# Gate and up projection of a decoder layer: 18 of 22 column blocks by seven partial products in place of eight

## The chip, the cores and the metric

The kernel runs on one core of one Trainium2 chip. The metric is the device time of one execution in microseconds, and the median of several runs stands for a kernel. The engines are TensorE (PE; its weight loads are listed as PEld), VectorE (DVE), ScalarE (ACT), GpSimd (POOL) and SyncE (SP), whose queue issues the transfers.

## The reference, cut to what matters

One inference step of a one-layer decoder for a prompt of 512 tokens and a sample group of 8 tokens, so 520 columns in all. The layer projects the normalised input, runs a matrix memory and a windowed attention, mixes them, projects the mix and normalises it. The change lies in what follows:

```python
x = layer_norm(ALPHA * x + mixed @ w_out, ln1_g, ln1_b)
g, u = jnp.split(x @ w_gate_up, 2, axis=-1)        # w_gate_up: 1024 x 5632, float32
ffn = (jax.nn.silu(g) * u) @ w_down                # w_down: 2816 x 1024
ple = jax.nn.sigmoid(x @ w_ple_gate) * (p @ w_ple)
x = layer_norm(ALPHA * x + ffn + ple, ln2_g, ln2_b)
```

All data is float32.

## The kernel before

**Layout.** Activations lie transposed: 128 of the 1024 channels on the partitions, 8 row tiles, 520 token columns. The columns are cut into `HALVES`: 264 (the 8 sample tokens and 256 of the prompt) and 256. A weight piece is 1024 x 128; a transfer of 1 MB brings a block of 256 weight columns, two pieces, into the ring `raw` (two buffers).

**Three products for one.** Every float32 operand is split into a high part (rounded to fp32r) and a low part (the rest). `split` makes the high part with an ACT copy (L190) and the low part with a DVE subtraction (L191). A product is the sum of high x high, high x low and low x high. `mm3` (L200) does that for one half of the columns, `mm3ab` (L217) for both in turn, with 3 x 8 x 2 = 48 matmuls for a piece. Split weights lie in the rings `whi` and `wlo` (three buffers each); `get` prepares pieces two ahead, and when a block's last piece is split, `load_next` asks for another block (L157).

**The stages around the change.** The output projection `w_out_half` runs for each half of the columns; on DVE L1253 and L1254 add the residual, and L1258 sums the rows for the mean. `Ln1` normalises a half: the mean matmul (L1271), `center` (L1277, and squares on ACT, L1282), `accum` (L1287), the variance matmuls (L1294), `rstd`, `diag`, `bcast` (L1317), then `final` (L1326 on DVE, the high part L1328 on ACT) and `final_lo`: for the row tiles in `LN1_POOL` ACT adds the bias into `d` (L1337) and POOL subtracts (L1338), for the others one DVE operation does both (L1340). The normalised activations x1 are `x1hi` and `x1lo`. The second half's normalisation is overlapped with `fill`, which starts the first five gate and up pieces on the first half's columns (L1392), and L1432 then does the first four pieces' other half.

**Gate and up.** There are 11 gate blocks and 11 up blocks, taken in turn: for each b the two gate pieces, then the two up pieces. `ev_g` takes a gate piece out of PSUM (tanh on ACT, L1135, and one DVE operation, L1369), `ev_u` an up piece (the product, L1375, then a split into `hhi`/`hlo`, the operands of the down projection). Then come the gate of the per-layer embeddings (`k_pg`, `base` holds their other factor, read back from `plesc` in one transfer of 2080 KB), the down projection, and the last normalisation with the stores.

**What sets the order.** A planner orders the instructions of each engine by its own model of time, except in the sections `tc.manual_schedule`, whose PE, DVE, ACT and POOL instructions keep the order in which they are written. Ahead of the change there are three such sections: the start, the second half of LayerNorm 1 with the fills, and the end.

Of the kernel before, what the change touches and what calls it, by code (L numbers as in the profile page):

```python
# [33 lines left out]
ALPHA = 2.0 ** 0.25  # L34
LN_EPS = 1e-5
RMS_EPS = 1e-6
KSC = float(P) ** -0.5
ASC = float(HD) ** -0.5
NEG = -1.0e30
# [9 lines left out]
def tile_hybrid_step(  # L49
# [98 lines left out]
    def load_next(part=0, parts=None):  # L148
        i = state["load"]
        if i >= len(blocks):  # L150
            return
        src, kc, ncol = blocks[i]
        if part == 0:
            raws[i] = ring("raw", 2048, 2)[:, : kc * ncol].rearrange("p (k n) -> p k n", k=kc)
        step = P if parts else ncol
        cs = slice(part * step, (part + 1) * step)
        nc.sync.dma_start(raws[i][:, :, cs], src[:, cs].rearrange("(k p) n -> p k n", p=P))  # L157
        if cs.stop >= ncol:
            state["load"] += 1

    def prep_next():
        i = state["prep"]
# [22 lines left out]
    def get(k, ahead=2):  # L185
        prep_to(k + ahead)
        return ready.pop(k)
# [75 lines left out]
    for b in range(4):  # L263
        add_block(w_out2[:, 256 * b : 256 * (b + 1)], KD, 256)
    k_gu = len(pieces)
    for b in range(11):
        add_block(w_gu2[:, 256 * b : 256 * (b + 1)], KD, 256)
        add_block(w_gu2[:, DFF + 256 * b : DFF + 256 * (b + 1)], KD, 256)
    k_pg = len(pieces)
    for b in range(4):  # L270
        add_block(w_pg[0][:, 256 * b : 256 * (b + 1)], KD, 256)
# [924 lines left out]
    for c0, kind, b in wl:  # L1196
        for a in range(2):
            f = 2 * b + a
            if t < 2:
                pa, pb = t01[t]  # L1200
            else:
                kp = kin[t]
                if t == 2:
                    after(prep_to, kp + 2, f_=mid)
                hi, lo = get(kp, 2 if kp + 2 < k_wo else k_wo - 1 - kp)
                pa, pb = psm(), psm()
                mm3ab((pa, pb), [(hi, lo, 0, KD, xhi, xlo, 0)])
            if kind == "qk":
                ev_qk(f, (pa, pb))
                if f == 7:  # L1210
                    G.memset(vaug()[:, :, :, DV : DV + 1], 1.0)
            elif kind == "mv":
                ev_mv(f, (pa, pb))
            elif kind == "k":
                (ev_ak if a == 0 else ev_av)((pa, pb))
            elif kind == "aq":
                ev_aq(f, (pa, pb))
            elif kind in ("mo", "gm"):
                ev_mo(f, (pa, pb))
            elif kind == "ga":  # L1220
                ev_ga(f, (pa, pb))
            sd.run(t)
            if t == 5:
                gates_tile()
            t += 1
        if kind == "gm" and b == 3:
            assert not sd.qs
            p1.__exit__(None, None, None)
            late = ctx.enter_context(tc.tile_pool(name="late", bufs=1))
            TL = [late.tile([P, U], F32, tag=f"L{k}", name=f"L{k}") for k in range(4)]  # L1230

            def sub8(t, k):
                return t[:, k * 1024 : (k + 1) * 1024].rearrange("p (k n) -> p k n", k=KD)

            for k in range(8):
                dest[k_wo + k] = (sub8(TL[k // 4], k % 4), sub8(TL[2 + k // 4], k % 4))

    T5, T6, T7, T8 = TL
    wo = [get(k_wo + k, 0) for k in range(8)]
    dest[k_gu + 3] = (sub8(T7, 0), sub8(T7, 1))  # L1240
    dest[k_gu + 4] = (sub8(T7, 2), sub8(T7, 3))

    rT = [qkT()[:, f, :] for f in range(KD)]
    x1hi, x1lo = xhi, xlo
# [18 lines left out]
    class Ln1:  # L1263
# [66 lines left out]
        def final_lo(self, f):  # L1330
            c0, n = self.c0, self.n
            d = rT[f][:, c0 : c0 + n]
            hi = x1hi[f][:, c0 : c0 + n]
            b1 = vecs[:, V_L1B + f : V_L1B + f + 1]
            lo = rr(x1lo[f][:, c0 : c0 + n])
            if f in LN1_POOL[self.hf]:
                S.activation(d, d, AF.Identity, bias=b1)  # L1337
                G.tensor_tensor(lo, d, hi, ALU.subtract)  # L1338
# [18 lines left out]
    for _ in range(5):  # L1357
        prep_next()

    hhi = [mxhi, mxlo, v3(slab(2))]  # L1360
    hlo = [v3(T5), v3(T6), v3(T7)]
    base4 = v34(late.tile([P, U], F32, tag="L3", name="base"))
    base = [base4[:, f, :] for f in range(KD)]
    nc.sync.dma_start(base4, plesc)

    def ev_g(psx, n):
        th = sig_gate(psx, n)
        t = ring("gt", 264, 5)
        V.scalar_tensor_tensor(t[:, :n], th[:, :n], 1.0, psx[:, :n], ALU.add, ALU.mult)  # L1369
        return t  # L1370

    def ev_u(f, hf, t, psx):
        c0, n = HALVES[hf]
        h32 = ring("tmp", 264, 4)
        V.scalar_tensor_tensor(h32[:, :n], t[:, :n], 0.5, psx[:, :n], ALU.mult, ALU.mult)  # L1375
        split(hhi[f // 8][f % 8][:, c0 : c0 + n], hlo[f // 8][f % 8][:, c0 : c0 + n], h32[:, :n])

    def part(w):
# [5 lines left out]
    with tc.manual_schedule(engines={E.PE, E.DVE, E.Pool, E.Activation}):  # L1384
        n0 = HALVES[0][1]
        pg = [psm() for _ in range(4)]

        def fill(q, k0, k1):
            hi, lo = g0[q]
            for k in range(k0, k1):  # L1390
                for i, (w, a) in enumerate(((hi, x1hi), (hi, x1lo), (lo, x1hi))):
                    T.matmul(  # L1392
                        pg[q][:, :n0], rr(w[:, k, :]), rr(a[k][:, :n0]),
                        start=(k == 0 and i == 0), stop=(k == KD - 1 and i == 2),
                    )
# [44 lines left out]
    for b in range(1, 11):  # L1440
        for a in range(4):
            q = 4 * b + a
            if b == 1 and a == 0:
                pp = (None, psm())
                mm3(pp[1], HALVES[1], part(g0[4]))
                ts[0, 0] = ts.pop((4, 0))
            else:
                w = get(k_gu + q)
                pp = (psm(), psm())
                mm3ab(pp, part(w))  # L1450
            for hf in range(2):
                if pp[hf] is None:
                    continue
                if a < 2:
                    ts[a, hf] = ev_g(pp[hf], HALVES[hf][1])
                else:
                    ev_u(2 * b + a - 2, hf, ts[a - 2, hf], pp[hf])

    for f in range(KD):
        w = get(k_pg + f)  # L1460
        p2 = (psm(), psm())
        mm3ab(p2, part(w))
        for psx, (c0, n) in zip(p2, HALVES):
# [232 lines left out]
```

## Time and profile before

| what | value |
|---|---|
| runs | 922.14, 919.64, 918.80 us; median 919.64 |
| profiled execution | 920.83 us, span 918.9 us, mean granted clock 0.989 |
| PE busy | 897.4 us, 98%, 7342 matmuls |
| DVE, ACT, POOL busy | 59%, 43%, 17% |
| transfers | 99.39 MB, mean 108 GB/s |

How to read the profile's lines: `L217` is line 217 of the kernel; `out<-in` names tiles with their buffer numbers left out (`psm` and `pss` are the two PSUM rings of four banks, `T` the large activation buffers, `L` the late ones); then the shape, the count, the busy time in us and the mean of one in ns. In a timeline the columns are the start and the length in us, and the square bracket gives the idle time ahead of an instruction on its engine and what ended it. Neighbouring instructions of one kind are merged.

### The profile page before, as it was taken

How to read it: one execution, taken by the hardware profiler on the slowest of the kernel's cores; microseconds unless marked ns; L12 is line 12 of the kernel's file. 1: busy time of each engine (PE TensorE's matmuls, PEld its weight loads, DVE VectorE, ACT ScalarE, POOL GpSimd, SP SyncE). 2: the span in 40 equal slices, each digit the busy share in tenths (PEclk: the TensorE clock that was granted, in tenths of full speed). 3: DMA queues.
4: the chain of work that ended last, by engine and by line, in shares of the span. 5: the costliest groups of instructions: out<-in, count | busy, mean ns of one | idle time of the engine just before them, and what ended most of it. 6: DMA issues, size and time to landing. Idle time of an engine off the chain costs nothing.

```text
span 918.9 us, 18329 instructions
## 1 busy us (share of the span) xinstructions
PE 897.4 (98%) x7342; PEld 885.6 (96%) x7342; DVE 545.5 (59%) x1367; ACT 397.5 (43%) x926; POOL 159.3 (17%) x320
## 2 busy tenths in 40 slices
PE   8999999999999999999999999999999999999994
PEld 7899999999999999999999999999999999999994
DVE  6788565788887768787875433333333355233327
ACT  5545355668777655565335222222222222122212
POOL 5441321125555211210022000000000000000004
PEclk9999999999999999999999999999999999999997
DMA  7542721544656431124421222222222223322212
GB/s 234 192 163 69 212 72 58 99 96 124 204 164 206 116 92 48 48 91 140 137 93 46 93 93 93 93 92 93 92 93 92 93 92 109 110 89 96 64 41 93
DMA packets 97731, 99.39 MB, mean 108 GB/s; under 512 B 5434, under 2 KB 93202, under 8 KB 97496
## 3 DMA queue, kind: packets, MB, share of 16 engines
q1 hardware_dynamic: 97216, 96.94, 34.0%
q8 instruction: 57, 0.93, 0.4%
q10 hardware_dynamic: 432, 1.31, 0.4%
q14 instruction: 26, 0.21, 0.1%
HBM read 89.01 MB, written 10.34 MB: 108 GB/s over the span
## 4 chain that ended last, share of the span: by engine, by line
PE 90%; DVE 5%; DMA 2%; ACT 1%; issue 1%; SPq 0%; POOL 0%; DVEq 0%; ACTq 0%
PE psm L217 69%; PE psm L200 6%; PE pss L650 2%; PE pss L703 1%; PE psm L1392 1%; PE pss L687 1%; PE psm L434 1%; PE pss L1036 1%; PE pss L1040 1%; DMA big<-vsd 1%; PE pss L1114 1%; PE pss L1432 1%; PE psm L1432 1%; DMA T<-in_w_ple_dram 1%; PE pss L1038 1%
## 5 line engine op out<-in xcount | busy, mean ns | idle before, releaser
L217 PE MATMUL psm<-T,whi 128*128 128x256 f32 (+1 forms) x3236 | 547.2, 284 | 0.0
L217 PEld LDWEIGHTS psm<-T,whi 128*128 128x128 f32 x3236 | 454.0, 188 | 1.9 <-PE pss L1114 0.3
L217 PE MATMUL psm<-T,wlo 128*128 128x264 f32 (+1 forms) x1716 | 362.9, 286 | 0.0
L217 PEld LDWEIGHTS psm<-T,wlo 128*128 128x128 f32 x1716 | 269.0, 188 | 0.6
L190 ACT ACTIVATE whi<-raw 128x1024 fp32r<-128x1024 f32 (+1 forms) x122 | 127.4, 1045 | 317.7 <-PE psm L217 258.6
L191 DVE TENSOR_TENSOR wlo<-raw,whi 128x1024 fp32r<-128x1024 f32 (+1 forms) x122 | 148.5, 1217 | 191.8 <-ACT whi L190 185.9
L1490 POOL COPY T<-tmp 128x8 f32<-128x8 f32 x8 | 1.5, 190 | 401.4 <-DVE tmp L1488 401.4
L217 PE MATMUL psm<-L,whi 128*128 128x264 f32 (+1 forms) x308 | 61.9, 282 | 0.0
L675 POOL TENSOR_SCALAR g<-g,sm 128x256 f32<-128x256 f32 (+1 forms) x64 | 37.2, 594 | 81.3 <-DVE sm L673 24.1
L1375 DVE SCALAR_TENSOR_TENSOR tmp<-gt,psm 128x264 f32<-128x264 f32 (+1 forms) x44 | 16.9, 421 | 57.6 <-PE psm L217 57.6
L200 PE MATMUL psm<-T,L 128*128 128x256 f32 (+1 forms) x280 | 49.5, 283 | 0.0
L217 PEld LDWEIGHTS psm<-L,whi 128*128 128x128 f32 x308 | 47.2, 188 | 0.0
L200 PEld LDWEIGHTS psm<-T,L 128*128 128x128 f32 x280 | 42.5, 188 | 0.0
L668 ACT ACTIVATE g<-g,sm 128x256 f32<-128x256 f32 (+1 forms) x64 | 30.2, 474 | 18.9 <-DVE sm L664 17.8
L1135 ACT ACTIVATE th<-psm 128x264 f32<-128x264 f32 x106 | 35.4, 378 | 5.5 <-DVE T L1142 2.4
L200 PE MATMUL psm<-S,L 128*128 128x264 f32 (+1 forms) x128 | 36.3, 286 | 0.0
L191 POOL TENSOR_TENSOR gt<-big,gt 128x256 fp32r<-128x256 f32 x32 | 27.6, 872 | 48.7 <-ACT gt L190 34.2
L659 DVE CUSTOM_DVE_ANT_0 g<-pss,amaskA,sink 128x256 f32<-128x256 f32 (+1 forms) x64 | 26.2, 446 | 4.6 <-PE pss L650 3.0
L217 PE MATMUL psm<-S,whi 128*128 128x264 f32 (+1 forms) x144 | 28.4, 288 | 0.0
L217 PE MATMUL psm<-S,wlo 128*128 128x264 f32 (+1 forms) x128 | 26.0, 285 | 0.0
L200 PEld LDWEIGHTS psm<-S,L 128*128 128x128 f32 x128 | 24.0, 188 | 0.0
L703 PE MATMUL pss<-big,VS 128*128 128x256 f32 x112 | 23.4, 304 | 0.0
(362 smaller groups left out, 1249.0 us busy)
## 6 DMA issues: line engine op xcount, KB each, us to landing
raw<-in_w_in_dram SPq DMA_DIRECT2D x24, 1024.0 KB
raw<-in_w_gate_up_dram SPq DMA_DIRECT2D x22, 1024.0 KB
raw<-in_w_down_dram SPq DMA_DIRECT2D x6, 1024.0 KB
big<-in_state_mlstm_C_dram SPq DMA_DIRECT2D x8, 512.0 KB
big<-vsd SPq DMA_DIRECT2D x8, 512.0 KB
out_dram<-big SPq DMA_DIRECT2D x8, 512.0 KB
raw<-in_w_out_dram SPq DMA_DIRECT2D x4, 1024.0 KB
raw<-in_w_ple_gate_dram SPq DMA_DIRECT2D x4, 1024.0 KB
```

What stands on the lines that cost most here:

```text
L190: S.activation(rr(hi), src, AF.Copy)
L191: (le or V).tensor_tensor(rr(lo), src, hi, ALU.subtract)
L200: T.matmul(ps[:, :n], rr(w[:, k, wc : wc + P]), rr(a[k0 + k][:, c0 : c0 + n]), start=(i == 0), stop=(i == tot - 1),)
L217: T.matmul(ps[:, :n], rr(w[:, k, wc : wc + P]), rr(a[k0 + k][:, c0 : c0 + n]), start=(i == 0), stop=(i == tot - 1),)
L650: T.matmul(sc[:, a, :w], rr(q[:, a, n * P : (n + 1) * P]), rr(KS[:, kv, hl, (n - 1 + k0) * P : (n + 1) * P]), start=(hl == 0), stop=(hl == 1),
L659: V.tensor_tensor_reduce(out=pr[:, a, :w], in0=sc[:, a, :w], in1=amaskA[:, k0 * P :], scale=1.0, scalar=sink8[:, 2 * j + a : 2 * j + a + 1 ...
L668: S.activation(pr[:, a, :w], pr[:, a, :w], AF.Exp, bias=sm[:, 2 + a : 3 + a], scale=ASC, accum_out=sm[:, 8 + a : 9 + a],)
L675: G.tensor_scalar(pr[:, a, :w], pr[:, a, :w], sm[:, 12 + a : 13 + a], 0.5, ALU.mult, ALU.mult)
L703: T.matmul(po[:, :256], rr(VS[:, n - 1 + k0 + b, kv, :]), rr(pp[:, x, b, :]), start=(i == 0), stop=(i == 2 * kb - 1),)
L1135: S.activation(th[:, :n], psx[:, :n], AF.Tanh, scale=0.5)
L1375: V.scalar_tensor_tensor(h32[:, :n], t[:, :n], 0.5, psx[:, :n], ALU.mult, ALU.mult)
L1432: T.matmul(pb4[q][:, :n1], rr(w[:, k, :]), rr(a[k][:, c1 : c1 + n1]), start=(k == 0 and i == 0), stop=(k == KD - 1 and i == 2),)
```

## The change

The gate and up blocks with b = 2 to 10, 18 blocks of 256 weight columns, are computed by one level of Strassen's algorithm in Winograd's form. The weight block is cut into 2 x 2 parts of 512 x 128, the activations into 2 x 2 parts of 512 channels x 260 columns. Seven products of these parts (12 matmuls of 260 columns each: 4 row tiles, 3 terms) replace eight. For each weight block DVE makes four sums of parts of 512 columns, and seven parts are split into high and low. The sums of x1 are made once, in place, and split (`TSTEPS`), written in block b = 1; for that `final_lo` leaves the whole of x1 in `d` for every row tile, with the bias added by ACT.

Partial results that two outputs share aren't added up on DVE: ACT copies a finished partial sum from one PSUM bank into another (a seed), and the next product accumulates on it. In the first two blocks one priming matmul goes ahead of a seed in each of the two banks concerned.

The loop over the 126 products is a section ordered by hand. In each iteration it writes the low part for four products ahead, the weight sum for six ahead, pending low parts of results, the harvest of the last product, seeds, the high part for five ahead, transfers, pending ACT work, and then the product. The products of one block overlap those of the next: s4 and a22 of a block come among the first of the next one.

Further edits: `ev_g` uses Silu on ACT alone, and `ev_u` a plain product; the weight blocks arrive as four transfers of 256 KB into slots of the two `raw` buffers; the last six tiles of the gated result stay unsplit until the `k_pg` stage; `base` comes back in eight transfers after the loop; two more row tiles of the fills (and the rest of the first piece) stand ahead of the mean matmul.

```diff
+BSW = 2
+TH = NT // 2
...
+    def st_load(g, n):
+        i = {"a11": 2 * g % 3, "a12": (2 * g + 1) % 3, "a21": 3 + g % 2, "a22": 5 + g % 3}[n]
...
+        nc.sync.dma_start(dst, sw[g][0][k0 * P : (k0 + 4) * P, c0 : c0 + P].rearrange("(k p) n -> p k n", p=P))
...
-            if f in LN1_POOL[self.hf]:
-                S.activation(d, d, AF.Identity, bias=b1)
-                G.tensor_tensor(lo, d, hi, ALU.subtract)
-            else:
-                V.scalar_tensor_tensor(lo, d, b1, hi, ALU.add, ALU.subtract)
+            S.activation(d, d, AF.Identity, bias=b1)
+            (G if f in LN1_POOL[self.hf] else V).tensor_tensor(lo, d, hi, ALU.subtract)
...
     def ev_g(psx, n):
-        th = sig_gate(psx, n)
         t = ring("gt", 264, 5)
-        V.scalar_tensor_tensor(t[:, :n], th[:, :n], 1.0, psx[:, :n], ALU.add, ALU.mult)
+        S.activation(t[:, :n], psx[:, :n], AF.Silu)
...
-        fill(0, 0, 5)
+        fill(0, 0, 8)
+        fill(1, 0, 2)
         lb.mean(accB)
-        fill(0, 5, 8)
+        fill(1, 2, 8)
...
-        fill(1, 0, 8)
...
+    TSTEPS = (
+        [(tsum, 0, j) for j in J4] + [(tsplit, 0, j) for j in J4] + [(tsum, 2, j) for j in J4],
+        [(tsum, 1, j) for j in J4] + [(tsplit, 1, j) for j in J4],
+        [(tsplit, 2, j) for j in J4] + [(tsum, 3, j) for j in J4],
+        [(tsplit, 3, j) for j in J4],
+    )
...
+    ORDER = (("a11", 0), ("s4", 1), ("s1", 0), ("s2", 0), ("a22", 1), ("a12", 0), ("s3", 0))
...
+    def w_sum(i):
+        g, form = steps[i]
+        if form in WBLK:
+            r = blk(g, form)
+        elif form == "s1":
+            r, s2f[g] = (ring("stg", NT, 2)[:, :512].rearrange("p (k n) -> p k n", k=4) for _ in range(2))
+            V.tensor_tensor(r, blk(g, "a21"), blk(g, "a22"), ALU.add)
+            V.tensor_tensor(s2f[g], blk(g, "a11"), r, ALU.add)
...
+    def prod(ps, g, form, start=True):
+        hi, lo = wf.pop((g, form))
+        xh, xl = TF[form]
+        for j in range(4):
+            for i, (w, x) in enumerate(((hi, xh), (hi, xl), (lo, xh))):
+                T.matmul(
+                    ps[:, :TH], rr(w[:, j, :]), rr(x[j]), start=(start and j == 0 and i == 0),
+                    stop=(j == 3 and i == 2), skip_group_check=not start,
+                )
...
+        if form == "a11":
+            pb, pa = pss(), pz[g, "a"]
+            pz[g, "b"] = pb
+            if g < 2:
+                prime(pb)
+            seed(lambda: S.activation(pb[:, :TH], pa[:, :TH], AF.Copy))
...
+    AHEAD = 5
+    ns = len(steps)
+    with tc.manual_schedule(engines={E.PE, E.DVE, E.Pool, E.Activation}):
+        for s in range(-AHEAD - 1, ns + 3):
+            if 0 <= s + AHEAD - 1 < ns:
+                w_lo(s + AHEAD - 1)
+            if s + AHEAD + 1 < ns:
+                w_sum(s + AHEAD + 1)
+            do(s, "dve")
+            if 0 < s <= ns:
+                harvest(s)
+            do(s, "seed")
+            if 0 <= s + AHEAD < ns:
+                w_hi(s + AHEAD)
+            elif ns - 3 <= s < ns:
+                prep_next()
+            st_loads(s)
+            do(s, "act")
+            if 0 <= s < ns:
+                product(s)
```

More of the change, by code (lines that the diff above doesn't have):

```diff
@@ L151, in load_next @@
             return
+        if blocks[i] is None:
+            state["load"] += 1
+            st_begin(i - k_sw)
+            return
         src, kc, ncol = blocks[i]
@@ L1358, in tile_hybrid_step @@
         prep_next()
[L1360 to L1364, printed above, removed]
+    hhi = [mxhi, mxlo]
+    hlo = [v3(T5[0]), v3(T6[0])]
     def ev_g(psx, n):
-        th = sig_gate(psx, n)
         t = ring("gt", 264, 5)
-        V.scalar_tensor_tensor(t[:, :n], th[:, :n], 1.0, psx[:, :n], ALU.add, ALU.mult)
+        S.activation(t[:, :n], psx[:, :n], AF.Silu)
         return t
@@ new lines, in tile_hybrid_step, with blk @@
+    ORDER = (("a11", 0), ("s4", 1), ("s1", 0), ("s2", 0), ("a22", 1), ("a12", 0), ("s3", 0))
+    steps = []
+    for g in range(len(sw) + 1):
+        for form, back in ORDER:
+            if 0 <= g - back < len(sw):
+                steps.append((g - back, form))
+    wf, s2f, nslot = {}, {}, [0]
+    wsrcs = {}
+    def blk(g, n):
+        return wblk[g, n]
+    def w_sum(i):
[6 more added lines that the diff above has]
+            V.tensor_tensor(s2f[g], blk(g, "a11"), r, ALU.add)
+        elif form == "s2":
+            r = s2f[g]
+        elif form == "s3":
+            r = blk(g, "a21")
+            V.tensor_tensor(r, blk(g, "a11"), r, ALU.add)
+        else:
+            r = blk(g, "a12")
+            V.tensor_tensor(r, r, s2f.pop(g), ALU.add)
+        wsrcs[i] = r
@@ new lines, in w_hi, with w_lo, st_loads @@
+    def w_hi(i):
+        nslot[0] += 1
+        t = ring(("whi", "wlo")[nslot[0] % 2], 1024, 3).rearrange("p (x k n) -> p x k n", x=2, k=4)
+        wf[steps[i]] = t[:, 0], t[:, 1]
+        S.activation(rr(t[:, 0]), wsrcs[i], AF.Copy)
+    def w_lo(i):
+        g, form = steps[i]
+        hi, lo = wf[g, form]
+        V.tensor_tensor(rr(lo), wsrcs.pop(i), hi, ALU.subtract)
+    def st_loads(s):
+        s += 2
+        for n, o in (("a22", 14), ("a21", 12), ("a11", 10), ("a12", 7)):
+            g = (s + o) // 7
+            if (s + o) % 7 == 0 and g < len(sw) and (g, n) not in wblk:
+                st_load(g, n)
+        if s in (7 * (len(sw) - 1) + 1, 7 * len(sw) + 1):
+            load_next()
@@ new lines, in prod, with prime @@
+    def prod(ps, g, form, start=True):
[7 more added lines that the diff above has]
+                )
+    def prime(ps):
+        T.matmul(ps[:, :TH], rr(x1hi[0][:, :P]), rr(x1hi[0][:, :TH]), start=True, stop=True)
@@ new lines, in tile_hybrid_step, with later, put_g, silu @@
+    todo = {}
+    def later(s, kind, f):
+        todo.setdefault((s, kind), []).append(f)
+    def put_g(s, b, r, hf, src, sc=1.0, own=None):
+        t = own or ring("gt", 264, 5)
+        ts[r, hf] = t
+        def silu():
+            S.activation(t[:, :TH], src, AF.Silu, scale=sc)
+        later(s if own is None else s + 1, "act", silu)
+    def put_h(s, b, r, hf, src, sc=1.0, own=None):
+        t = ts.pop((r, hf))[:, :TH]
+        f, c0 = 2 * b + r, hf * TH
+        if f >= 16:
+            h = h6[f - 16][:, c0 : c0 + TH]
+        else:
+            h = (own or ring("tmp", 264, 4))[:, :TH]
+        V.scalar_tensor_tensor(h, src, sc, t, ALU.mult, ALU.mult)
+        if f < 16:
+            hi, lo = (x[f // 8][f % 8][:, c0 : c0 + TH] for x in (hhi, hlo))
+            later(s + 1, "act", lambda: S.activation(rr(hi), h, AF.Copy))
+            later(s + 2, "dve", lambda: V.tensor_tensor(rr(lo), h, hi, ALU.subtract))
@@ new lines, in tile_hybrid_step, with product @@
+    pz = {}
+    def product(s):
+        g, form = steps[s]
+        if form == "a11":
+            pz[g, "a"] = psm()
+            prod(pz[g, "a"], g, form)
+        elif form == "s1":
+            pz[g, "c"] = pss()
+            prod(pz[g, "c"], g, form)
+        elif form == "s2":
+            prod(pz[g, "b"], g, form, start=False)
+        elif form == "a12":
+            prod(pz[g, "a"], g, form, start=False)
+        elif form == "s3":
+            prod(pz[g, "d"], g, form, start=False)
+        elif form == "s4":
+            prod(pz[g, "c"], g, form, start=False)
+        elif form == "a22":
+            prod(pz[g, "d"], g, form, start=False)
@@ new lines, in do @@
+    def do(s, kind):
+        for f in todo.pop((s, kind), ()):
+            f()
+    AHEAD = 5
[18 more added lines that the diff above has]
+                product(s)
```

125 lines of the change are left out of this document (116 added, 9 removed).

## The prediction, made before the changed kernel was built or run

> **What bounds the kernel now.** First the page: busy shares, and the slices of the span.
>
> ```profile
> span 918.9 us, 18329 instructions
> PE 897.4 (98%) x7342; PEld 885.6 (96%) x7342; DVE 545.5 (59%) x1367; ACT 397.5 (43%) x926; POOL 159.3 (17%) x320
> ...
> DVE  6788565788887768787875433333333355233327
> ACT  5545355668777655565335222222222222122212
> POOL 5441321125555211210022000000000000000004
> PEclk9999999999999999999999999999999999999997
> ```
>
> PE is busy 98% of the span; from the 23rd slice on, where the change lies, DVE stands at 3 tenths and ACT at 2. Busy matmuls alone prove little, since they are pipelined, so next comes the chain that ended last, in order of time, and the busy time in chosen stretches.
>
> ```profile
> 421.74 27.42 PE psm L200 x226
> 449.61 10.08 PE psm L200 x85
> ...
> 499.68 2.84 PE psm L200 x24
> 502.52 301.14 PE psm L217 x2507
> ```
>
> ```profile
> 464.00:475.00 11.00, 9.15 (x75) 8.89 (x74) 9.96 (x22) 5.56 (x14) 4.06 (x5) 1.00 0.36 126
> 485.00:502.00 17.00, 17.00 (x146) 17.00 (x145) 7.47 (x16) 10.94 (x24) 6.04 (x8) 1.00 0.01 1
> 547.00:593.00 46.00, 46.00 (x385) 46.00 (x384) 18.25 (x32) 13.17 (x24) 0.00 (x0) 1.00 0.28 93
> 856.00:887.00 31.00, 31.00 (x261) 31.00 (x260) 10.05 (x18) 7.26 (x11) 0.38 (x2) 1.00 0.26 77
> 887.00:919.00 32.00, 19.46 (x153) 18.21 (x152) 19.38 (x47) 6.58 (x13) 9.87 (x11) 0.80 0.18 67
> ```
>
> (Columns: stretch, its length, busy PE, weight load, DVE, ACT, POOL, granted clock, DMA share, GB/s.) From 502.52 on the chain is one unbroken run of matmuls: 301.14/2507 = 120.1 ns each, at 260 columns on average (264 and 256 in turn). In 547:593 PE never idles and DVE has 28 us of 46 free. So here a removed matmul is worth 120.1 ns, as long as DVE and ACT can feed PE.
>
> **The change, part by part.**
>
> *Matmuls.* A block of 256 weight columns takes 2 pieces x 48 = 96 matmuls of 260 columns on average. Seven products of 4 row tiles x 3 terms make 84 of 260. 18 blocks x 12 fewer = 216, x 120.1 ns = -25.9 us. Four priming matmuls come back: +0.5. That each matmul now has weights of its own costs nothing: L200 in the rows above runs one half at a time, with new weights for each matmul, at 121.3 ns (264 columns) and 118.6 (256), mean 120.0. The Trainium skill (TensorE: Matmul & The Clock Gate, Back-to-back issue gap) gives N/2.4 + 2.5 ns for a warm matmul by itself, an estimate of 110.8 ns at 260 columns; by it the 216 would be worth 23.9 us. The rows measure 9 ns more, and the sum goes by them.
>
> *The loop's DVE and ACT work.* Prices:
>
> ```profile
> L390 DVE TENSOR_TENSOR g<-T,g 128x512 fp32r<-128x512 f32 x2 | 1.3, 696 | 0.0
> L1375 DVE SCALAR_TENSOR_TENSOR tmp<-gt,psm 128x264 f32<-128x264 f32 x22 | 9.4, 427 | 57.6 <-PE psm L217 57.6
> L387 ACT ACTIVATE g<-T 128x512 fp32r<-128x512 f32 x2 | 1.1, 618 | 0.0
> L1135 ACT ACTIVATE th<-psm 128x264 f32<-128x264 f32 x54 | 20.3, 378 | 2.6 <-PE psm L217 2.1
> L190 ACT ACTIVATE T<-tmp 128x264 fp32r<-128x264 f32 x14 | 5.7, 410 | 1.1 <-DVE tmp L1375 1.1
> L131 ACT ACT_TABLE_LOAD x1 | 1.3, 1283 | 0.7 <-PEq L1683 0.7
> ```
>
> ```profile
> 40.28 0.69 DVE L390 TENSOR_TENSOR g<-T,g 128x512 fp32r<-128x512 f32 x1
> ...
> 40.89 0.70 DVE L390 TENSOR_TENSOR g<-T,g 128x512 fp32r<-128x512 f32 x1
> ...
> 561.04 1.23 DVE L191 TENSOR_TENSOR wlo<-raw,whi 128x1024 fp32r<-128x1024 f32 x1 [0.21 <-ACT whi L190]
> 562.19 0.76 DVE L191 TENSOR_TENSOR L<-tmp,T 128x264 fp32r<-128x264 f32 x2
> ```
>
> Durations overlap their neighbours: two 264-wide operations take 0.76 us, so the second adds 0.34, and two 512-wide ones start 0.61 apart. A gate block and its up block together need on DVE: 14 low parts and 8 weight sums of 512, and of 260 columns 2 combinations for the gate, 2 combinations, 4 products and 4 low parts for up: 22 x 0.61 + 12 x 0.34 = 17.5 us (22 x 0.696 + 12 x 0.427 = 20.4 if nothing overlapped). PE needs 168 x 0.1201 = 20.2 us for the pair. ACT: 14 x 0.618 + 12 x 0.378 (8 seeds and saved copies, 4 Silu) + 4 x 0.410 = 14.8. So DVE goes from 4 tenths to about 87%, near the limit but under it, and 4 operations lighter in the last three up blocks, which leave the split for later.
>
> The cover is the order. Low parts are issued four products ahead of their matmuls: 4 x 12 x 0.1201 = 5.8 us. The worst stretch on DVE is the first four products after an up block: 4 low parts, 4 weight sums and about 6 operations of 260 columns: 8 x 0.61 + 6 x 0.34 = 6.9 us against 5.8 us of PE. The lag of 1.1 us fits into the lead, and the next three products (4.3 us) carry only about 2.5 us. Each iteration issues the weight work ahead of the harvest, the operation that waits for PE; behind a waiting harvest stands the next low part, with those four products in hand. A seed is read by the second or third product after it: 2.9 us for a copy that the trace has only from PSUM into SBUF (0.38); PSUM to PSUM I take as that; at 0.618, the dearest copy above, it is still in time, and a cheaper one gains nothing. On ACT, too, the seed waits for PE with the high part for five products ahead behind it. Stalls inside the loop: 0 to 2, I take 0.5.
>
> *Weight loads.* The same bytes arrive as 72 transfers of 256 KB with 512-byte rows in place of 18 of 1 MB with 1024-byte rows, 1 MB per 10.1 us = 104 GB/s. With 1024-byte rows 93 GB/s took a share of 0.28; in 856:887, which fetches the 128-column blocks of w_down in 512-byte rows, 77 GB/s took 0.26. By that 104 GB/s take 0.35. A block is asked for at least five iterations (7.2 us) before its high part is made, and SP has only these transfers to issue. Nothing on the path; a late one would stop ACT's queue first, PE four products later.
>
> *Silu for tanh and one DVE operation.* It frees DVE, which was not the bound: 0. It adds at most one table load, 1.28 us, on ACT about 479, where ACT then waits until 485.33 (next fence): 0, or +1.3 without that cover.
>
> *LayerNorm 1 and the fills.*
>
> ```profile
> 469.83 0.40 PE L1392 MATMUL psm<-T,whi 128*128 128x264 f32 x2
> ...
> 470.32 2.54 POOL L1338 TENSOR_TENSOR T<-T,T 128x264 fp32r<-128x264 f32 x3 [1.27 <-ACT T L1337]
> ...
> 469.74 1.32 ACT L1337 ACTIVATE T<-T,vecs 128x264 f32<-128x264 f32 x3
> ...
> 485.33 1.31 ACT L1328 ACTIVATE T<-T,vecs 128x256 fp32r<-128x256 f32 x3 [5.92 <-DVE T L1326]
> ```
>
> ```profile
> 473.65 0.70 PE L1271 MATMUL pss<-gt,onesD 128*128 128x256 f32 x2 [1.85 <-DVE gt L1258]
> ...
> 478.56 0.83 DVE L1287 TENSOR_TENSOR gt<-gt,tmp 128x256 f32<-128x256 f32 x2 [0.21 <-ACT tmp L1282]
> ...
> 481.10 0.95 PE L1294 MATMUL pss<-onesD,gt 128*128 128x1 f32 x8
> ```
>
> PE stood idle 1.85 us ahead of the mean (the only idle in 464:475). 15 more matmuls (1.82 us) now precede it. Three additions on ACT (0.41 us apart) put the last high and low parts of half 0 back by 1.2 us, to 472.3 on ACT and about 473.1 after POOL, so fill 0, which reaches its last row tile at 469.83 + 21 x 0.121 = 472.4, may wait some 0.6 us there; the mean comes 0.45 us later and PE has 1.82 us more behind it: -1.4 (ends -1.85 and 0). The variance then is reached 1.4 us earlier, at 479.8, about when its squares are summed (479.4 + 0.45): the slack of 1.7 us is used up, and nothing later than this sum becomes late.
>
> *Sums and splits of x1, and the way into the loop.* 16 sums and 16 low parts on DVE, 32 x 0.34 = 10.9 us, and 16 copies on ACT, 6.6 us. They go into the idle 9.5 us of DVE in 485:502 and the 3.5 pieces after it (20.2 us, with some 12 us of work of their own). Whether the planner may slip them between instructions of a section ordered by hand shows at 32 us:
>
> ```profile
> 32.12 0.41 DVE L359 TENSOR_TENSOR T<-tmp,T 128x256 fp32r<-128x256 f32 x1
> ...
> 32.58 1.63 DVE L191 TENSOR_TENSOR wlo<-raw,whi 128x1024 fp32r<-128x1024 f32 x1
> 34.13 0.48 DVE L354 CAST T<-tmp 128x256 fp32r<-128x256 f32 x2
> ```
>
> L359 and L354 belong to such a section, L191 doesn't, so it may; the first splits of the loop can likewise run beside the last pieces. If not, the 20 sums and low parts written ahead of the third piece's split cost 20 x 0.34 - 2.84 (the half piece that PE still has) = 4.0 us. Ends 0 and +4; I take +1, nearer the rows above.
>
> *The way out.* Three preparations in the last three iterations, eight loads of 260 KB in place of one of 2080, six splits of 520 columns (0.7 us on DVE) beside pieces of 5.8 us: hidden; ends 0 and +2, taken +0.5. The tail is the same.
>
> Sum: -25.9 + 0.5 + 0.5 - 1.4 + 1.0 + 0.5 = -24.8. The profiled execution took 920.83 (span 918.9 and 1.93 around it), 1.19 over the median of the three runs; 919.64 - 24.8 = 894.8.
>
> **The rivals.**
>
> *DVE becomes the bound.* If durations don't overlap, a pair takes 20.4 against 20.2: +2 us in nine pairs, 897. If in addition each of the 12 narrow operations waits 0.21 us for its releaser, as at 561.04, a pair takes 22.9: +24 us, and nothing is gained. Against it: that wait ended a copy issued immediately before, while here one iteration lies between. Middle: 906.
>
> *The x1 work blocks the way in.* +4 us, and up to 2 more for the first low parts of the loop: 899.
>
> *Slower: pauses between products bring down the granted clock.* The last row of the stretches has PE busy 19.46 of 32 us and the clock at 0.80. At 0.80 the loop's 1512 matmuls (181.6 us) would take 227: +45, 940. It decides below a clock of 0.88 over the loop. Against it: in 485:502 PE went round four banks in groups of three matmuls with 17.00 us busy of 17.00 and the clock at 1.00. The Trainium skill (TensorE: Matmul & The Clock Gate, A second HAM failure mode: psum-queue depth-cycling) warns of just this, short idles between groups that cycle through the banks. By that row the trace doesn't bear it out, so its chance is small.
>
> *The change doesn't do what it says: a matmul costs more than 120 ns.* Its moving columns now start at multiples of 1040 bytes; all starts so far were multiples of 32 bytes, so no row shows it. 6 ns each cost 9 us (904); at 16 ns the gain is gone.
>
> **How the numbers follow.** Forecast 0.62 (own range 892 to 897); way in 0.15; DVE bound 0.14; dearer matmuls 0.04; clock 0.05. The range: 891, the floor of the sum (919.64 - 25.9 + 0.5 - 1.85 = 892.4) and 1 us of spread between runs, to 906, which takes in the way in and half of the DVE case: about 0.82. A change of 0.5% (4.6 us) is about what can be told from none. Faster 0.90 (the first three but the upper end of DVE, and most of the fourth), same 0.04, slower 0.06 (clock, and the dearest matmuls).
>
> **What would show it.** Right: some 216 fewer matmuls net of the primes, 120 ns each in the loop, PE full and the clock at 1.00 there, DVE 8 to 9 tenths, no idle ahead of the mean matmul. Wrong: PE idle released by a DVE low part inside the loop (DVE the bound), idle about 502 to 520 released by DVE (way in), matmuls over 125 ns, or a clock under 1.00.

## The result, and the profile after

The changed kernel takes 897.88 us (median of 4 runs) against 920.68 before (4 runs, the three of the table and one more); the ratio is 0.9756, with a 95% interval from 0.9725 to 0.9788. The forecast was 894.8, in a range from 891 to 906. The profiled execution took 900.21 us, its span 898.2.

The page of the changed kernel, lines as shown of before:

```profile
span 898.2 us, 18486 instructions
PE 873.0 (97%) x7130; PEld 860.3 (96%) x7130; DVE 637.4 (71%) x1547; ACT 466.6 (52%) x1102; POOL 159.2 (18%) x320
...
DVE  7788555688888777778877978999988654223327
ACT  6545254657777655557326656666665522212212
POOL 5441321115464411311014100000000000000004
PEclk9999999999999999999999999999999999999997
```

DVE now stands at 7 to 9 tenths in the slices of the loop, ACT at 5 to 6; the granted clock reads as before. The chain that ended last, in order of time, from the way into the loop to the way out:

```profile
503.89 1.04 ACT whi L216
505.20 0.95 ACT whi L216
506.87 1.15 DVE wlo L217
508.06 17.28 PE psm L243 x142
525.34 1.43 PE psm L1600 x12
526.89 2.88 PE pss L1600 x24
...
704.23 1.45 PE pss L1600 x12
705.68 1.69 PE psm L243 x14
707.37 1.45 PE psm L1600 x12
708.82 74.58 PE psm L243 x621
```

L1600 is the matmul of the seven products (`prod`). From 525 to 709 the chain is PE alone, as it was before; 14 matmuls of the next stage (1.69 us) have slipped in ahead of the last product. Outside it, one stretch of ACT and DVE stands on the chain at 504 to 508: the way into the loop. A window inside the loop (columns as above):

```profile
530.00:700.00 170.00, 170.00 (x1420) 170.00 (x1419) 150.65 (x276) 110.96 (x246) 0.00 (x0) 1.00 0.37 106
```

PE has no idle, DVE is busy for 89%, ACT for 65%. (The last three pairs of blocks, which leave the split for later, begin in this window. Four full pairs, 565.94 to 646.54, take 80.60 us, with DVE busy for 73.16: 18.3 us of 20.15 for a pair.)

Since the start of the program varies from execution to execution (last section), the comparisons below measure from the first fill matmul (469.83 us before, 474.24 after) to the end of the span: the **stretch**. It took 449.07 us before and 423.96 after: 25.1 us less. Ahead of it this execution lost 4.4 us, and the spans differ by the rest, 20.7. The parts, in us:

| part of the stretch | before | after |
|---|---|---|
| first fill matmul to the second half's matmuls | 18.41 | 17.78 |
| second half's matmuls | 11.28 | 11.28 |
| from there to the first product (before: 24 + 144 matmuls, 2.84 + 17.29) | 20.13 | 21.87 |
| from there to the end | 399.25 | 373.03 |

### The profile page after: what moved, and what is told of

The parts are those of the page before. It is cut to its first block, busy times and chain, and to the rows that moved or that the text cites. A ratio compares the mean times of both kernels' runs of the same rounds, so it can differ in the third digit from the quotient of the medians.

```text
span 898.2 us, 18486 instructions
## 1 busy us (share of the span) xinstructions
PE 873.0 (97%) x7130; PEld 860.3 (96%) x7130; DVE 637.4 (71%) x1547; ACT 466.6 (52%) x1102; POOL 159.2 (18%) x320
## 4 chain that ended last, share of the span: by engine, by line
PE 85%; DVE 6%; DMA 3%; ACT 3%; issue 1%; POOL 1%; SPq 0%; DVEq 0%; ACTq 0%; POOLq 0%
PE psm L243 46%; PE psm L1600 12%; PE pss L1600 9%; PE psm L226 6%; PE pss L683 2%; DMA big<-vsd 1%; PE psm L467 1%; PE pss L736 1%; PE pss L720 1%; PE psm L1428 1%; PE pss L1069 1%; PE pss L1073 1%; ACT T L1371 1%; DMA out_dram<-stg 1%; DMA T<-in_w_ple_dram 1%
## 5 line engine op out<-in xcount | busy, mean ns | idle before, releaser
L243 PE MATMUL psm<-T,whi 128*128 128x264 f32 x2000 | 346.5, 286 | 0.6 <-DVE Qbd L670 0.4
L243 PEld LDWEIGHTS psm<-T,whi 128*128 128x128 f32 x2000 | 284.7, 189 | 2.6 <-PE pss L1147 0.6
L243 PE MATMUL psm<-T,wlo 128*128 128x264 f32 (+1 forms) x1056 | 230.0, 288 | 1.5 <-DVE wlo L217 1.5
L217 DVE TENSOR_TENSOR wlo<-raw,whi 128x1024 fp32r<-128x1024 f32 (+1 forms) x86 | 104.8, 1218 | 107.2 <-ACT whi L216 106.8
L243 PEld LDWEIGHTS psm<-T,wlo 128*128 128x128 f32 x1056 | 168.1, 189 | 2.4 <-DVE wlo L217 1.7
L216 ACT ACTIVATE whi<-raw 128x1024 fp32r<-128x1024 f32 (+1 forms) x86 | 89.1, 1038 | 154.5 <-PE psm L243 139.6
L243 PE MATMUL psm<-L,whi 128*128 128x264 f32 x224 | 45.0, 282 | 0.0
L1584 DVE TENSOR_TENSOR whi<-raw,whi 128x512 fp32r<-128x512 f32 x45 | 30.9, 687 | 8.5 <-ACT whi L1579 7.6
L1584 DVE TENSOR_TENSOR wlo<-raw,wlo 128x512 fp32r<-128x512 f32 x45 | 30.9, 686 | 3.7 <-ACT wlo L1579 3.3
L1600 PE MATMUL psm<-tf,whi 128*128 128x260 f32 x228 | 30.3, 282 | 0.0
L1600 PE MATMUL psm<-T,wlo 128*128 128x260 f32 x216 | 28.9, 283 | 0.0
L1600 PE MATMUL pss<-tf,whi 128*128 128x260 f32 x216 | 28.9, 283 | 0.0
L1600 PE MATMUL pss<-tf,wlo 128*128 128x260 f32 x216 | 28.9, 283 | 0.0
L1600 PE MATMUL psm<-T,whi 128*128 128x260 f32 x216 | 28.9, 283 | 0.0
```

The lines of the kernel that those rows point to most:

```text
L216: S.activation(rr(hi), src, AF.Copy)
L217: (le or V).tensor_tensor(rr(lo), src, hi, ALU.subtract)
L243: T.matmul(ps[:, :n], rr(w[:, k, wc : wc + P]), rr(a[k0 + k][:, c0 : c0 + n]), start=(i == 0), stop=(i == tot - 1),)
L1584: V.tensor_tensor(rr(lo), wsrcs.pop(i), hi, ALU.subtract)
L1600: T.matmul(ps[:, :TH], rr(w[:, j, :]), rr(x[j]), start=(start and j == 0 and i == 0), stop=(j == 3 and i == 2), skip_group_check=not start,)
```

## The experiments

The table gives the four parts for every run, as the timelines of their traces have them; its first column is where the stretch began.

| run | begins | to second half | second half | to first product | from there | stretch |
|---|---|---|---|---|---|---|
| before | 469.83 | 18.41 | 11.28 | - | - | 449.07 |
| changed | 474.24 | 17.78 | 11.28 | 21.87 | 373.03 | 423.96 |
| silu_only | 470.71 | 18.41 | 11.28 | - | - | 448.79 |
| ten_blocks | 473.07 | 17.78 | 11.29 | - | - | 435.83 |
| preps_first | 470.01 | 17.79 | 11.28 | 20.11 | 373.01 | 422.19 |
| fills_old | 470.79 | 17.27 | 11.28 | 21.91 | 372.95 | 423.41 |
| dve2 | 471.02 | 17.75 | 11.28 | 21.89 | 373.36 | 424.28 |
| dve4 | 473.26 | 17.78 | 11.28 | 21.88 | 396.80 | 447.74 |
| ahead3 | 472.77 | 17.77 | 11.28 | 21.90 | 372.88 | 423.83 |
| ahead2 | 471.06 | 17.79 | 11.28 | 21.88 | 373.09 | 424.04 |
| ahead1 | 474.00 | 17.77 | 11.28 | 21.91 | 401.74 | 452.70 |
| ln1_only | 474.91 | 17.29 | 11.28 | - | - | 448.09 |
| both_edits | 473.78 | 17.28 | 11.29 | 20.11 | 373.04 | 421.72 |
| after_again | 473.44 | 17.80 | 11.28 | 21.90 | 372.98 | 423.96 |

Where an edit doesn't touch a part, that part repeats within 0.1 us (from the first product on within 0.25): differences far below the spread of whole runs can be read here. The span is read to 0.1 us, so the last two columns are good to 0.05. The ratios below are each against runs of before made beside them. `fills_old`, `ln1_only`, `dve2`, `dve4` and `ahead1` to `ahead3` are one execution each; of them only the parts are compared.

**Is the gain the removed matmuls?** Two runs: one part of the change alone in the kernel before, and the whole change with fewer blocks.

```diff
     def ev_g(psx, n):
-        th = sig_gate(psx, n)
         t = ring("gt", 264, 5)
-        V.scalar_tensor_tensor(t[:, :n], th[:, :n], 1.0, psx[:, :n], ALU.add, ALU.mult)
+        S.activation(t[:, :n], psx[:, :n], AF.Silu)
...
-        V.scalar_tensor_tensor(h32[:, :n], t[:, :n], 0.5, psx[:, :n], ALU.mult, ALU.mult)
+        V.tensor_tensor(h32[:, :n], t[:, :n], psx[:, :n], ALU.mult)
```

> The kernel before with one part of the change alone: Silu in place of tanh and a DVE operation, in all 22 blocks. Theory (PE is the bound, DVE had room): the time from the first fill matmul to the end of the span stays at 449 us, give or take 0.5, and the ratio to before is 1.000. Rival (part of the gain comes from DVE operations saved): that stretch is 2 us or more shorter.

Measured: ratio 0.9995 (0.9973 to 1.0017), stretch 448.79, 0.3 less than before. That 0.3 lies at the very end: from the tenth-last matmul to the end of the span it is 12.55 us before (12.68 in `ln1_only`), and 12.24 to 12.31 in every run with Silu; the cause is open. Up to there fewer DVE operations are worth nothing: DVE had room.

```diff
-BSW = 2
+BSW = 6
```

> The changed kernel with 10 blocks by seven products in place of 18; the other 8 go by eight products. Theory (the gain is 12 matmuls of 120 ns per block, 1.44 us, on top of costs that don't depend on the number of blocks): the stretch from the first fill matmul to the end is 8 x 1.44 = 11.5 us longer than the 424.0 of the changed kernel, 435.5, and the time is near 909. Rival (the loop pays per block for stalls, or the gain lies elsewhere): the difference is clearly under 11.5 us, and the time stays under 905.

Measured: 911.27 us, 2 more than the 909 expected, ratio 0.9859 (0.9838 to 0.9879); stretch 435.83 against the 435.5 expected, 11.9 longer than with 18 blocks, 1.48 us for each of the eight. The gain goes by blocks, at the price of 12 matmuls each (1.44). The remaining 13.2 us of gain are 10 blocks at that price less the costs that don't grow with their number.

**The way into the loop.** PE's timeline in the changed kernel:

```profile
506.14 0.40 PE L243 MATMUL psm<-T,whi 128*128 128x264 f32 x2
508.06 0.39 PE L243 MATMUL psm<-T,wlo 128*128 128x264 f32 x1 [1.52 <-DVE wlo L217]
```

The piece's first two terms need only the high part; the third waits for the low part. DVE had worked from 488.6 on without a pause, most of it on sums and low parts of x1. The edit queues the later ones behind this piece's split:

```diff
             if b == BSW - 1:
+                if a == 0:
+                    prep_to(k_gu + 5)
+                    first = list(last_split)
                 for f, i, j in TSTEPS[a]:
-                    f(i, j)
+                    if a == 0:
+                        f(i, j)
+                    else:
+                        after(f, i, j, f_=first)
```

(`last_split` holds the two instructions of the last split, and `after` orders what follows behind them.)

> The changed kernel with the split of the sixth gate and up piece written ahead of the sums and splits of x1, and the last 20 of the sums and low parts queued behind it. Theory (PE's idle at 506 us, which ends with that piece's low part, comes from the x1 work ahead of it on DVE and ACT): the idle of 1.5 us goes and the stretch from the first fill matmul to the end is 1.5 to 1.9 us shorter, 422.3. Rival (the piece waits for its buffers or its weights): the idle stays.

Measured: the wait is gone, and the part takes 20.11 us, the time of its 168 matmuls; the stretch is 1.77 us shorter. The time is 895.39 us, ratio 0.9695 (0.9673 to 0.9717). Its DVE timeline has the split first:

```profile
499.24 1.23 DVE L217 TENSOR_TENSOR wlo<-raw,whi 128x1024 fp32r<-128x1024 f32 x1 [2.13 <-PE psm L1470]
500.38 1.44 DVE L1493 SCALAR_TENSOR_TENSOR T<-T 128x260 f32<-128x260 f32 x4
```

The split did wait for a buffer, until matmuls of the second half (L1470) let it go, but its low part then began 2.7 us ahead of the piece's first matmul (501.92). So the buffers and the weights are there in time; the order of the x1 work was the cause.

**LayerNorm 1 and the fills.**

```diff
-        fill(0, 0, 8)
-        fill(1, 0, 2)
+        fill(0, 0, 5)
         lb.mean(accB)
-        fill(1, 2, 8)
+        fill(0, 5, 8)
...
+        fill(1, 0, 8)
```

> The changed kernel with the fills around the mean matmul in their old order (five row tiles ahead of it). Theory (the new order hides the wait for the sum of rows): PE idles ahead of the mean matmul again by 1 to 2 us, and the start of the second half's matmuls comes 0.5 to 1.5 us later after the first fill matmul than the 17.7 us of the changed kernel. Rival (the sum is in time either way): no change.

The expectation failed. The second half's matmuls start 17.27 us after the first fill, 0.5 earlier than in the changed kernel, and PE waits only 0.33 us ahead of the mean, for a low part and not for the sum. The two PE timelines, changed kernel and old order:

```profile
474.24 0.40 PE L1428 MATMUL psm<-T,whi 128*128 128x264 f32 x2
...
476.43 0.40 PE L1428 MATMUL psm<-T,whi 128*128 128x264 f32 x1 [0.31 <-POOL T L1380]
...
477.31 0.39 PE L1428 MATMUL psm<-T,whi 128*128 128x264 f32 x1 [0.25 <-POOL T L1380]
...
479.29 0.59 PE L1314 MATMUL pss<-gt,onesD 128*128 128x256 f32 x2
```

```profile
472.97 0.39 PE L1428 MATMUL psm<-T,whi 128*128 128x264 f32 x1 [0.33 <-POOL T L1380]
473.20 0.29 PE L1428 MATMUL psm<-T,wlo 128*128 128x264 f32 x1
473.32 0.63 PE L1314 MATMUL pss<-gt,onesD 128*128 128x256 f32 x2
```

With the new order PE meets two late low parts (0.56 us of idle) ahead of the mean, and the mean comes 5.05 us after the first fill in place of 2.53: 30 matmuls precede it, which alone take 30 x 0.121 = 3.6 us, in place of 15. So something else had taken away the old wait of 1.85 us. The kernel before with the LayerNorm edit alone tells what:

```diff
-            if f in LN1_POOL[self.hf]:
-                S.activation(d, d, AF.Identity, bias=b1)
-                G.tensor_tensor(lo, d, hi, ALU.subtract)
-            else:
-                V.scalar_tensor_tensor(lo, d, b1, hi, ALU.add, ALU.subtract)
+            S.activation(d, d, AF.Identity, bias=b1)
+            (G if f in LN1_POOL[self.hf] else V).tensor_tensor(lo, d, hi, ALU.subtract)
```

> The kernel before with one part of the change alone: in LayerNorm 1 ACT adds the bias for every row tile and the low part is a plain subtraction. Theory (the plain subtraction and the planner's new order on DVE, not the order of the fills, bring the sum of rows earlier): the sum is ready about 2.4 us after the first fill matmul in place of 3.8, and the second half's matmuls start 17.3 us after it in place of 18.4. Rival (the order of the fills was needed): 18.4 or more.

Measured: 17.29 and, from its DVE timeline, a sum ready 477.30 - 474.91 = 2.4 us after the first fill:

```profile
475.66 0.42 DVE L1337 TENSOR_TENSOR T<-T,T 128x264 fp32r<-128x264 f32 x1
476.00 0.41 DVE L1254 SCALAR_TENSOR_TENSOR T<-T,T 128x256 f32<-128x256 f32 x1
476.45 0.85 DVE L1258 TENSOR_TENSOR gt<-gt,T 128x256 f32<-128x256 f32 x1
477.23 0.97 DVE L1337 TENSOR_TENSOR T<-T,T 128x264 fp32r<-128x264 f32 x1
```

The last low part on DVE now comes after the sum (L1258); before, all three (L1340) came ahead of it, the last of them so:

```profile
470.33 1.04 DVE L1340 SCALAR_TENSOR_TENSOR T<-T,vecs,T 128x264 fp32r<-128x264 f32 x1
...
473.17 0.42 DVE L1258 TENSOR_TENSOR gt<-gt,T 128x256 f32<-128x256 f32 x1
```

The edit that was made to leave x1 in `d` brought the gain, and its order on DVE is what the timelines show changed; no run has the old operation in the new order. The fills' new order gives half of the gain back: `both_edits` repeats the 17.27 of `fills_old` with 17.28.

**How near DVE is to its limit.** Low parts of some forms are subtracted twice, with the same result:

```diff
-        V.tensor_tensor(rr(lo), wsrcs.pop(i), hi, ALU.subtract)
+        src = wsrcs.pop(i)
+        for _ in range(2 if form in ("a11", "s1") else 1):
+            V.tensor_tensor(rr(lo), src, hi, ALU.subtract)
```

> The changed kernel with the low parts of two of the seven weight forms (a11 and s1) subtracted twice: two more 512-wide DVE operations per block. Theory (operations cost their start to start time, 0.61 us, and the order covers them): a pair of blocks needs 17.5 + 4 x 0.61 = 19.9 us of DVE against 20.2 of PE, so the stretch from the first product to the end stays within 1.5 us of the 373.0 of the changed kernel. Rival (full durations or waits make DVE the limit): 20.4 + 4 x 0.696 = 23.2 us for a pair, +27 us over nine pairs.

> The changed kernel with the low parts of four of the seven forms (a11, s1, a22, s3) subtracted twice. Theory (DVE has some 13% to spare and no more): 17.5 + 8 x 0.61 = 22.4 us for each of six pairs and about 21 for the last three, against 20.2 of PE, so DVE is the bound and the stretch from the first product is about 16 us longer, 389. Rival (neighbouring operations overlap further, DVE has much room): under 3 us longer.

(`dve4` has the forms a11, s1, a22 and s3.) Measured: +0.3 us with two, +23.8 with four. The same window with two and with four:

```profile
530.00:700.00 170.00, 169.97 (x1416) 169.76 (x1416) 165.86 (x306) 110.03 (x244) 0.00 (x0) 1.00 0.36 106
```

```profile
530.00:700.00 170.00, 155.98 (x1249) 150.81 (x1249) 167.02 (x301) 96.85 (x217) 0.00 (x0) 1.00 0.31 89
```

With two, DVE at 98% costs PE nothing. With four it is busy for 98% again, but now it is the bound, as four pairs of blocks in the middle of the loop of `dve4` show:

```profile
567.00:661.40 94.40, 84.56 (x675) 81.38 (x674) 92.74 (x169) 53.61 (x120) 0.00 (x0) 1.00 0.31 90
```

A pair takes 23.6 us, and DVE is busy for 23.2 of them. Prices from start to start are right with two (79.53 us of DVE in four pairs of `dve2`, 19.9 for a pair, as priced) and 0.8 us low with four (22.4); full durations would have been 23.2 and 26.0. That 0.8, and 0.4 in which DVE stands idle, make the loss larger than the 16 us expected. PE doesn't wait for DVE directly there, but for ACT; the waits of PE and then of ACT in 530:700 of `dve4`:

```profile
PE psm L1602 <- ACT psm L1681: 13.5, 13, 1.7
```

```profile
ACT wlo L1579 <- DVE raw L1572: 12.2, 7, 1.9
ACT S L1634 <- DVE tmp L1631: 10.7, 12, 1.4
ACT wlo L1579 <- DVE raw L1569: 10.0, 7, 2.6
```

L1681 is the seed of the bank on which s3 and a22 accumulate. It stands on ACT's queue behind a high part that waits for a late weight sum (L1569, L1572).

**How much lead the loop needs.**

```diff
-    AHEAD = 5
+    AHEAD = 2
...
-            st_loads(s)
+            st_loads(s - 3)
```

(`ahead3`: 3 and s - 2. `ahead1`: 1 and s - 4, with one more iteration at the end.)

> The changed kernel with the weight work three products ahead in place of five (low parts two products, 2.9 us, ahead in place of four; weight transfers shifted with them). Theory (the lead only has to cover the lag of about 1.1 us behind an up block and one copy and one subtraction): the stretch from the first product is within 1 us of 373.0. Rival (the four-product lead is needed): 5 us longer or more.

> The changed kernel with the weight work two products ahead (low parts one product, 1.44 us, ahead). Theory (DVE's spare 13% doesn't help when its lag isn't covered): PE waits for low parts behind up blocks, and the stretch from the first product is 3 to 15 us longer than 373.0. Rival (with DVE below its limit any lead will do): within 1 us.

> The changed kernel with the weight work one product ahead, so that a low part is made during the product just before its own. Theory (a lead of one product is all that the loop needs, and one is needed: a seed, a high part and a low part one after another take 0.4 + 0.6 + 0.7 us and more against the 1.44 us of a product): PE waits at most products for a low part, and the stretch from the first product is 20 to 100 us longer than 373.0. Rival (no lead is needed): within 1 us.

Measured, from the first product on: 372.88, 373.09 and 401.74 us. With the low parts two products ahead nothing changes, as expected; with one product nothing changes either, against the expectation; with none that part is 28.7 us longer, some 25 of it in the loop. (The rest lies right behind the loop, where this edit also puts off the splits of the next pieces: PE waits 1.24 us for one at 734.59.) The window in `ahead1`:

```profile
530.00:700.00 170.00, 161.30 (x1244) 152.32 (x1244) 133.19 (x244) 95.13 (x218) 0.00 (x0) 1.00 0.32 92
```

PE's waits in the same window (us in total, times, longest):

```profile
PE pss L1600 <- DVE whi L1584: 5.3, 7, 0.8
PE psm L1600 <- DVE whi L1584: 1.5, 7, 0.2
```

PE is idle for 8.7 of the 170 us, where the changed kernel leaves none, and most of it ends with L1584, with DVE busy for only 78%: the low part comes late although DVE has room. The idle isn't the whole price: PE did 1244 matmuls here in place of 1420, 21 us of work at 120 ns. The rest lies within what counts as busy; the weight loads (PEld) wait 16.0 us for L1584 in this window. One turn of it, each line behind the one above:

```profile
607.58 0.39 ACT L1673 ACTIVATE th<-pss 128x260 f32<-128x260 f32 x1 [1.59 <-PE pss L1600]
607.86 0.62 ACT L1579 ACTIVATE whi<-raw 128x512 fp32r<-128x512 f32 x1
608.51 0.69 DVE L1584 TENSOR_TENSOR whi<-raw,whi 128x512 fp32r<-128x512 f32 x1 [1.36 <-ACT whi L1579]
609.26 1.27 PEld L1600 LDWEIGHTS psm<-tf,whi 128*128 128x128 f32 x10 [0.25 <-DVE whi L1584]
```

ACT's copy of a finished product waits for PE, the high part of the next weights stands behind it on ACT, and the low part, which waits for the high part, is then late for the product that needs it.

**Both edits together**, `preps_first` and `fills_old`, beside the changed kernel on the same chip:

> The changed kernel with two edits: the sixth piece's split ahead of the x1 work, and the fills around the mean matmul in their old order. Theory (the two gains, 1.77 and 0.55 us, lie at different places and add): the stretch from the first fill matmul to the end is 421.6 us, and the time about 2.3 us under the changed kernel's. Rival (the earlier second half only lengthens the wait on the way into the loop): 422.2 as with the first edit alone.

> The changed kernel once more, beside the one with both edits. Expected: 424.0 us (within 0.4) from the first fill matmul to the end of the span, whatever the start of that stretch, which lay between 469.8 and 474.2 us in ten executions with the same order of instructions ahead of it; ratio to before 0.972 to 0.979.

Measured: 895.14 us, ratio to before 0.9712 (0.9682 to 0.9742), and 897.14 us, 0.9733 (0.9707 to 0.9760). The stretches are 421.72 and 423.96: the two gains add to 2.24 us. In whole runs the intervals overlap; the parts of the stretch tell the difference.

## Why the prediction was right

The bound was read rightly: PE before, PE after, and the gain is the matmuls that went. The stretch came out close to the sum, but in part by luck: several terms were off, and their errors cancelled. By the steps of the sum:

- **Matmuls, -25.9 and +0.5.** Right. From the first product (525.17) to 707.13 (708.82 less the 1.69 us that slipped in) 1512 + 4 matmuls took 181.96 us, 120.0 ns each; the 1728 that they replace took 1728 x 120.1 ns = 207.5. That is 25.5 us less, against 25.4 forecast. The dearer matmuls of the fourth rival did not come: starts at multiples of 1040 bytes cost nothing. The estimate of 110.8 ns from the Trainium skill (TensorE: Matmul & The Clock Gate, Back-to-back issue gap) is missed by the same 9 ns as before.
- **DVE and ACT in the loop, +0.5.** Stalls were 0. The 87% for DVE became 89% in the window and 91% (18.3 us in place of 17.5) in a full pair; ACT's 73% became 65%, because that sum used full durations (a full pair keeps ACT busy for 13.5 us in place of 14.8). `dve2` and `dve4` bear out that the limit is near.
- **"The cover is the order."** Four products of lead carry the loop, as the step says, but they aren't needed: a lead of one product is enough (`ahead2`), none isn't (`ahead1`). The step's figures for the lag were too careful, which cost the forecast nothing.
- **Weight loads.** 104 GB/s at a share of 0.35 was expected; 106 at 0.37 was found, and no wait of PE.
- **Silu: 0.** Right up to the last 12.5 us of the program, where 0.3 went (`silu_only`). The table load took 1.28 us at 484.40, while ACT had nothing else to do.
- **LayerNorm 1 and the fills, -1.4.** It brought -0.63, and the step failed in its mechanism. It gave the gain to the 15 matmuls ahead of the mean and took the added bias operations for a cost; `ln1_only` and `fills_old` show the reverse, -1.1 from the edit of the bias and the subtraction and +0.5 from the fills' order. The wait of some 0.6 us for late low parts that it allowed for did come (0.56).
- **The way in, +1.0.** It cost 1.74, between the ends 0 and 4.0. The mechanism is the one named, x1 work ahead of the split of the piece that PE needs next (the sixth piece; the prediction's text calls it the third), and `preps_first` shows it by taking it away. The planner did slip x1 work into the section ordered by hand, from 492 on, but put the rest of it ahead of the split. Idle about 502 to 520 released by DVE, one of the signs of being wrong, so did show: 1.52 us.
- **The way out, +0.5.** PE had no idle there; the cost was 0. From the first product to the end the difference is 26.2 us (399.25 less 373.03), 0.7 more than the matmuls account for. 0.5 of it shows behind the loop: the last 1400 matmuls start 181.07 us ahead of the end in place of 181.55. The 0.3 at the very end is part of it; the sum has no such term.

The sum came to -24.8, and the stretch gave -25.1. That the two agree within 0.3 us is luck: LayerNorm 1 brought 0.8 less than its term and the way in cost 0.7 more, and the stalls and the way out, which cost nothing in place of 0.5 each, and the 0.7 us just named made up for it. The medians differ by 22.8; the interval of the ratio, applied to 920.68, holds savings from 19.5 to 25.3 us. In the profiled executions what the spans lack against the stretch is the start of the program (4.4 us); the other runs of the result have no trace to show it. Beside each other a second time, with 6 and 11 runs, the medians differ by 25.1 us (897.14 and 922.25). The range allowed 1 us for the spread of runs; runs of the changed kernel lay between 894.96 and 900.21.

Of the rivals, DVE as the bound did not come, but `dve4` shows how near it was; its middle is put at 906, where its own ends, 897 and 919, give 908. The granted clock stayed at 1.00 through the loop: groups of 12 matmuls that go round eight banks brought no pause. The warning of the Trainium skill (TensorE: Matmul & The Clock Gate, A second HAM failure mode: psum-queue depth-cycling) has no case here.

## What to carry to other kernels

Where PE runs without a gap and other engines have room, a removed matmul is worth its place in the stream (120 ns here), and what has to be counted is whether the work put on DVE and ACT instead stays under PE's time, at prices from start to start. A lead of one product was enough to hide it. A busy share of 98% doesn't tell on which side of the limit DVE is: nothing was lost while its work for a pair of blocks stayed under PE's (19.9 against 20.2 us), 23.8 us were when it passed it (23.2), and the loss showed as a wait for ACT, whose queue stood behind DVE. An edit made for one purpose can earn its gain through the order that the planner then chooses, so each part is worth a run alone, read on a part of the trace that the rest doesn't touch.

## What the runs showed that was not expected

The time ahead of the stretch was between 469.83 and 474.91 us in 14 profiled executions whose engines ran the same instructions in the same order up to the output projection, just ahead of it; after that point each part repeated within 0.4 us wherever the kernel had not been changed. Both ends of that range are kernels without the seven products (`before`, `ln1_only`), so it is no effect of the change. Three windows of before, and the same of the changed kernel:

```profile
70.00:110.00 40.00, 38.73 (x321) 37.68 (x320) 30.03 (x68) 17.81 (x33) 10.67 (x22) 1.00 0.43 124
200.00:250.00 50.00, 49.98 (x414) 49.06 (x413) 42.45 (x132) 40.34 (x118) 25.64 (x48) 1.00 0.54 149
300.00:350.00 50.00, 49.83 (x411) 48.22 (x412) 35.92 (x119) 30.18 (x87) 8.69 (x19) 1.00 0.32 92
```

```profile
70.00:110.00 40.00, 36.92 (x293) 35.86 (x292) 28.05 (x66) 17.53 (x31) 9.57 (x20) 0.96 0.45 125
200.00:250.00 50.00, 48.72 (x401) 47.55 (x400) 42.26 (x134) 38.34 (x114) 21.82 (x44) 1.00 0.57 153
300.00:350.00 50.00, 48.67 (x401) 47.04 (x399) 36.07 (x119) 31.33 (x90) 11.14 (x22) 1.00 0.37 111
```

By the starts of the same matmuls the changed kernel was 2.0 us ahead at 95 us, 1.3 behind at 110, 2.8 behind at 254 and 4.4 behind from 310 on. So these three windows hold its three losses, 6.4 us together, and the first 40 us had given it 2.0. PE's busy time is 4.2 us less in them, which is not all of the loss; in the first the granted clock was 0.96 in place of 1.00. What delayed PE there is open.

A second point: an fp32 copy by ACT from one PSUM bank into another (128x260) took 0.372 us, as much as one into SBUF (0.384 to 0.388), and matmuls that went on accumulating on a bank filled so ran at the same 120 ns.
